# Issuing three groups of DRAM writes from GpSimd instead of SyncE in a two-layer trunk kernel

## Chip, cores and metric

The kernel runs on 1 core of one Trainium2 chip. The time is that of one execution on the device in microseconds (us). Five engines take part: TensorE (PE, with its weight loads shown as PEld), VectorE (DVE), ScalarE (ACT), GpSimd (POOL) and SyncE (SP), which here does nothing but issue DMAs.

## The reference

One layer of a streaming-encoder trunk, batch 1, 512 tokens, width 2048, hidden width 8192, all in float32. What matters here is the second half:

```
x = layer_norm(ALPHA * x + g1 * mix, ln1_g, ln1_b)      # mix: three parallel head groups
h = x * (1.0 + sc2) + sh2
ff = square(relu(h @ w_ff1)) @ w_ff2                    # 2048 -> 8192 -> 2048
x = layer_norm(ALPHA * x + g2 * ff, ln2_g, ln2_b)
```

## The kernel before

Each float32 matmul is made of three matmuls on split operands: a value is written once rounded (`wh`, by ACT) and once as the rest (`wl`, by DVE, which reads `wh`), and PE adds up wh·xh, wl·xh and wh·xl. The helper `split` does both; `act` (L57), `tt` (L60), `stt` (L63) and `load` (L127) record nearly all instructions of their engines, so one line of the profile stands for many places.

**Order.** The program doesn't write out the order of the engines' queues. A planner places the instructions of each engine before the run, by priorities (`prio`, the table `PRIO`) and by its own costs, and puts in the waits. On the chip each queue then runs strictly in that order: an instruction that waits holds up everything behind it on its engine. SP's queue holds all loads and nearly all writes; POOL's holds four `memset` (L220) and the 24 accumulating DMAs of L1365.

**First layer norm** (L993 to L1012, 870 to 960 us). Four token tiles are normalised, transposed and modulated. The modulated tile goes to `hx_d`, the normalised residual `r1[:, t]` (1 MB a tile) to `xn_d`; `base` reads `xn_d` again much later, in the second layer.

**First MLP layer** (`ff1_unit`, 960 to 1616 us). 16 blocks of 512 hidden columns. The first is done plainly, the other 15 by Strassen's scheme: seven products a block (`strassen`), each of two halves `c`, and each half of 24 matmuls on one `wh`/`wl` pair (three buffers each). A block's weights come in four loads of 1 MB into `raw`, which has four buffers: a buffer is free for the next block when the last `wl` that reads it is made. Before the products that need sums of weights, `form` makes them on DVE into `st`.

The products' results are made into four quarters `ev` (relu, square). `quarter_done` and `sums_done` put seven tiles a block into the list `waiting`, and `spread` takes one of them after each product: `put` splits it into an `hc` tile (two buffers; ACT writes the upper half, DVE the lower) and writes it, 512 KB, to `hc_d`. There are 14 such blocks. The quarters of the last two blocks are written as they are to `h_d` (256 KB, eight writes).

**Second MLP layer** (`ff2_unit` and after, from 1605 us) loads `hc_d` into `hin` (L1327), and `wff2` into `raw`; `base` loads `xn_d` into `y` (L1298). Its POOL DMAs (L1365) add a tile onto `ffa`.

The lines that the change touches:

```
nc.sync.dma_start(xn_d[t], r1[:, t])                                        # L1012
nc.sync.dma_start(hc_d[e, ORDER.index(name), :, c], w.bitcast(F32))         # L1063, in put
nc.sync.dma_start(h_d[b - 2 * NS][:, 2 * i:2 * i + 2, ...], quad2(o))       # L1081, in quarter_done
```

Of the kernel before, what the change touches and what calls it, by code (L numbers as in the profile page):

```python
# [10 lines left out]
F32 = mybir.dt.float32  # L11
# [40 lines left out]
def trunk_kernel(ctx, tc, A, out):  # L52
    nc = tc.nc
    V, S, G, T = nc.vector, nc.scalar, nc.gpsimd, nc.tensor

    def act(o, i, f=AF.Copy, **kw):
        S.activation(o, i, f, **kw)  # L57
# [7 lines left out]
    def ts(o, a, s1, s2, op0, op1=None):  # L65
        if op1 is None:
            V.tensor_scalar(o, a, s1, None, op0=op0)
        else:
            V.tensor_scalar(o, a, s1, s2, op0=op0, op1=op1)
# [11 lines left out]
    def prio(name):  # L81
        if name not in PRIO:
            name += str(stage_no[0])
        return tc.high_priority(offset=PRIO[name])

    def bank(n="mm"):
        if "two" in pools:
            return two_banks()[:, 0]
        return pools[n].tile([128, 512], F32, name=n)
# [30 lines left out]
    def split(h, l, src):  # L120
        act(h, src)
        tt(l, src, h.bitcast(F32), OP.subtract)
# [302 lines left out]
    with prio("index"):  # L425
# [23 lines left out]
        for t in range(3):  # L449
# [10 lines left out]
            for hf in range(2):  # L460
                ps = bank("sa")
                for j in range(4):
                    o = (4 * hf + j) * 128
# [465 lines left out]
    r1 = R.tile([128, NT, D], F32, name="r1")  # L929
# [13 lines left out]
    for nb in range(4):  # L943
# [17 lines left out]
        for t in range(NT):  # L961
          with prio("wo"):
            o = r1[:, t, nb * 512:(nb + 1) * 512]
# [11 lines left out]
    def ln_scalars(t):  # L975
        V.bn_aggr(out=mv[:, t, 0:2], in_=stats[:, t].rearrange("p a b -> p (a b)"))
        act(mv[:, t, 2:3], mv[:, t, 1:2], AF.Sqrt, bias=eps[:, 1:2])
        V.reciprocal(mv[:, t, 2:3], mv[:, t, 2:3])
        stt(mv[:, t, 3:4], mv[:, t, 0:1], -1.0, mv[:, t, 2:3], OP.mult, OP.mult)
# [3 lines left out]
    xn_d = dram.tile([NT, 128, D], F32, name="xn_d")  # L983

    NE, NS = 8, 7
    hc_d = dram.tile([NS, 7, 128, 2, 2, 2, 256], F32, name="hc_d")
    h_d = dram.tile([16 - 2 * NS, 128, 4, SEQ], F32, name="h_d")
# [4 lines left out]
    with prio("ln1"):  # L992
        for t in range(NT):  # L993
            ln_scalars(t)
            act(r1[:, t], r1[:, t], AF.Identity, scale=mv[:, t, 2:3], bias=mv[:, t, 3:4])
            tk = slice(t * 128, (t + 1) * 128)
            for kq in range(4):
                ps = bank(("sa", "sb")[kq % 2])
                for j in range(4):
                    k = 4 * kq + j  # L1000
                    T.transpose(ps[:, j * 128:(j + 1) * 128], r1[:, t, k * 128:(k + 1) * 128], ident)
                hf = WO.tile([128, 4, 128], F32, name="hf2", bufs=3)
                for j in range(4):
                    k = 4 * kq + j
                    o = ps[:, j * 128:(j + 1) * 128]
                    if j % 2 == 0:
                        act(hf[:, j], o, AF.Identity, scale=mod2[:, 0, k:k + 1], bias=mod2[:, 1, k:k + 1])
                    else:
                        ts(hf[:, j], o, mod2[:, 0, k:k + 1], mod2[:, 1, k:k + 1], OP.mult, OP.add)
                split(acts[:, 4 * kq:4 * kq + 4, 0, tk], acts[:, 4 * kq:4 * kq + 4, 1, tk], hf)  # L1010
                nc.sync.dma_start(hx_d[:, 4 * kq:4 * kq + 4, tk], hf)
            nc.sync.dma_start(xn_d[t], r1[:, t])  # L1012
    wo.close()
    adap.close()
    res.close()
# [39 lines left out]
    ORDER = ("b11", "b21", "n2", "t3", "n1", "t4", "b22")  # L1055

    def put(b, name, o):

        e, c = divmod(b, 2)
        w = ST.tile([128, 2, 2, 256], F32R, name="hc", bufs=2)  # L1060
        with prio("hc"):
            split(w[:, 0], w[:, 1], quad2(o))
            nc.sync.dma_start(hc_d[e, ORDER.index(name), :, c], w.bitcast(F32))  # L1063

    waiting = []

# [5 lines left out]
    def quad2(o):  # L1072
        return o.rearrange("p (m n) -> p m n", m=2)

    def quarter_done(b, i, j, o):
        if b < 2 * NS:
            if (i, j) != (0, 1):
                waiting.append(lambda: put(b, f"b{i + 1}{j + 1}", o))
        else:
            with prio("ff1"):  # L1080
                nc.sync.dma_start(h_d[b - 2 * NS][:, 2 * i:2 * i + 2, 256 * j:256 * j + 256], quad2(o))  # L1081

    def sums_done(b, o):

        if b >= 2 * NS:
            return
        b11, b22, b21, b12 = o

        def sub(dst, x, y, neg=False):
            with prio("hc"):  # L1090
                if neg:
                    stt(dst, x, -1.0, y, OP.mult, OP.subtract)
                else:
                    tt(dst, x, y, OP.subtract)

        def piece(name, *args):
            sub(*args)
            put(b, name, args[0])

        for args in (("n1", b11, b11, b12), ("t3", b12, b22, b12), ("n2", b22, b11, b22, True),  # L1100
                     ("t4", b21, b22, b21, True)):
            waiting.append(lambda args=args: piece(*args))

    o4 = []
    for i, j in QUARTERS:
        r = ev_tile()
        with prio("ff1"):
            for m in range(2):
                act(r[:, 256 * m:256 * m + 256], banks[2 * i + m][:, 256 * j:256 * j + 256], AF.Relu)
            act(r, r, AF.Square)  # L1110
        quarter_done(0, i, j, r)
        o4.append(r)
# [95 lines left out]
    def ff1_unit(b):  # L1208
# [22 lines left out]
        def done(i, j, o, ps, neg=False):  # L1231

            with prio("ff1"):
                if o is None:
                    o = ev_tile()
                    act(o, ps, AF.Relu)
                else:
                    tt(o, ps, o, OP.add)
                    act(o, o, AF.Relu, scale=-1.0 if neg else 1.0)
                act(o, o, AF.Square)  # L1240
            part[i, j] = o
            quarter_done(b, i, j, o)
# [220 lines left out]
    e = NE - 1  # L1463
# [13 lines left out]
    for t in range(NT):  # L1477
# [7 lines left out]
        for q in range(4):  # L1485
            cs_ = slice(512 * q, 512 * q + 512)
            o = ffa[:, t, cs_]
# [94 lines left out]
```

## Time and profile before

| what | value |
|---|---|
| median of 3 runs | 2275.1 us (2272.95 to 2275.82) |
| the profiled execution | 2272.37 us, of which its span 2270.6 us |
| PE busy | 2158.4 us, 95% of the span |
| DVE busy | 1876.2 us, 83% |
| ACT busy | 1098.1 us, 48% |
| POOL busy | 44.6 us, 2% |
| mean granted TensorE clock | 0.989 of full speed |
| SP's queue | 471.04 MB, 56.9% of the 16 DMA engines' time |
| POOL's queue | 12.58 MB, 3.3% |

The span runs from the first to the last instruction; the profiled execution has 1.8 us around it. An engine's queue that is blocked can be seen as a wait of the instruction at its head; a DMA has a time of issue and, where the trace has it, a time from issue to landing.

### The profile page before, as it was taken

The page shows a single profiled execution, that of the slowest core. Times are in us where ns is not written, and L with a number is a line of the kernel's source. Part 1 is how long each engine was busy: PE and PEld are TensorE (multiplying, and loading weights), DVE is VectorE, ACT ScalarE, POOL GpSimd, SP SyncE. Part 2 cuts the span into 40 slices and gives each one's busy share as a digit, 9 for nine tenths or more (in the row PEclk, how much of TensorE's full clock was granted, in tenths as well). Part 3 has the DMA queues.
Part 4 walks back from the last instruction along what each step waited for, and adds up shares of the span by engine and source line. Part 5 has one row for each costly group of instructions (what it writes and reads, how often), then busy time and mean ns, then how long its engine had stood idle before and what let it go on. Part 6 is the DMA issues. An engine that isn't in the chain of part 4 may idle for free.

```text
span 2270.6 us, 30604 instructions
## 1 busy us (share of the span) xinstructions
PE 2158.4 (95%) x11947; PEld 1845.2 (81%) x11947; DVE 1876.2 (83%) x2520; ACT 1098.1 (48%) x1572; POOL 44.6 (2%) x55
## 2 busy tenths in 40 slices
PE   6999999988889999999999999999999999999997
PEld 4778887866666787899899999999888887878886
DVE  7896899998776876788778778777699988998788
ACT  3332444448766223666555555555444443444432
POOL 0000000000000000000000000000000000000000
PEclk9999999999999999999999999999999999999999
DMA  8877563254234676735544554554788988796562
GB/s 318 315 295 288 174 228 117 95 202 151 82 107 135 239 288 254 252 135 207 202 178 177 194 185 168 204 186 142 295 307 259 342 276 275 243 333 234 149 239 86
DMA packets 129625, 485.58 MB, mean 214 GB/s; under 512 B 15556, under 2 KB 38468, under 8 KB 88264
## 3 DMA queue, kind: packets, MB, share of 16 engines
q1 hardware_dynamic: 122952, 471.04, 56.9%
q0 software_dynamic: 6528, 12.58, 3.3%
q8 instruction: 94, 1.54, 0.3%
q14 instruction: 51, 0.42, 0.1%
HBM read 392.35 MB, written 78.64 MB: 207 GB/s over the span
## 4 chain that ended last, share of the span: by engine, by line
PE 41%; DVE 34%; DMA 15%; ACT 5%; issue 4%; DVEq 0%; SPq 0%; ACTq 0%
DMA raw<-in_wff_dram 11%; DVE wl L60 11%; DVE st L60 4%; PE two L1348 4%; PE mm L197 4%; PE two L1349 4%; PE mm L198 4%; PE two L1347 4%; PE mm L196 4%; PE mm L210 3%; PE mm L208 3%; PE mm L209 3%; DVE ffa L60 2%; DVE raw L60 2%; DVE adaz L63 2%
## 5 line engine op out<-in xcount | busy, mean ns | idle before, releaser
L57 ACT ACTIVATE wh<-raw 128x1024 fp32r<-128x1024 f32 x332 | 349.2, 1057 | 408.8 <-PE two L1349 146.3
L60 DVE TENSOR_TENSOR wl<-raw,wh 128x1024 fp32r<-128x1024 f32 x332 | 402.4, 1218 | 59.8 <-ACT wh L57 59.3
L1348 PE MATMUL two<-wl,hin 128*128 128x512 f32 x784 | 309.2, 394 | 5.4 <-DVE wl L60 5.2
L1347 PE MATMUL two<-wh,hin 128*128 128x512 f32 x784 | 307.4, 392 | 3.8 <-ACT wh L57 2.1
L1349 PE MATMUL two<-wh,hin 128*128 128x512 f32 x784 | 306.8, 391 | 0.0
L203 PE MATMUL mm<-acts,wl 128*128 128x256 f32 x720 | 208.6, 290 | 23.8 <-DVE wl L60 23.8
L196 PE MATMUL mm<-acts,wh 128*128 128x512 f32 (+1 forms) x568 | 221.6, 394 | 7.2 <-ACT ve L57 3.8
L197 PE MATMUL mm<-acts,wl 128*128 128x512 f32 (+1 forms) x568 | 223.3, 393 | 1.1 <-DVE wl L60 0.9
L198 PE MATMUL mm<-acts,wh 128*128 128x512 f32 (+1 forms) x568 | 221.2, 390 | 0.0
L63 DVE SCALAR_TENSOR_TENSOR adaz<-raw,cols,adaz 128x1024 f32<-128x1024 f32 (+2 forms) x180 | 198.1, 1111 | 11.7 <-DMA raw<-in_adaR_dram 8.8
L202 PE MATMUL mm<-acts,wh 128*128 128x256 f32 x720 | 204.9, 285 | 1.7 <-ACT ev L57 1.7
L204 PE MATMUL mm<-acts,wh 128*128 128x256 f32 x720 | 204.8, 284 | 0.0
L203 PE MATMUL mm<-tx,wl 128*128 128x256 f32 x720 | 203.9, 283 | 0.0
L204 PE MATMUL mm<-tx,wh 128*128 128x256 f32 x720 | 203.2, 282 | 0.0
L202 PE MATMUL mm<-tx,wh 128*128 128x256 f32 x720 | 202.0, 281 | 0.0
L1348 PEld LDWEIGHTS two<-wl,hin 128*128 128x128 f32 x784 | 147.9, 189 | 45.6 <-DVE wl L60 14.5
L1347 PEld LDWEIGHTS two<-wh,hin 128*128 128x128 f32 x784 | 147.9, 189 | 36.1 <-ACT wh L57 3.0
L209 PE MATMUL mm<-wl,acts 128*128 128x512 f32 x448 | 175.0, 391 | 1.2 <-DVE wl L60 1.0
L210 PE MATMUL mm<-wh,acts 128*128 128x512 f32 x448 | 174.9, 391 | 0.0
L208 PE MATMUL mm<-wh,acts 128*128 128x512 f32 x448 | 174.1, 392 | 0.3 <-DVE z_t L60 0.2
L1349 PEld LDWEIGHTS two<-wh,hin 128*128 128x128 f32 x784 | 148.0, 189 | 30.2
L203 PEld LDWEIGHTS mm<-acts,wl 128*128 128x128 f32 x720 | 139.2, 193 | 30.9 <-DVE wl L60 30.7
(316 smaller groups left out, 4534.9 us busy)
## 6 DMA issues: line engine op xcount, KB each, us to landing
raw<-in_wff_dram SPq DMA_DIRECT2D x128, 1024.0 KB, 6.7
hc_d<-hc SPq DMA_DIRECT2D x98, 512.0 KB, 4.2
hin<-hc_d SPq DMA_DIRECT2D x49, 1024.0 KB, 9.0
raw<-in_adaR_dram SPq DMA_DIRECT2D x48, 1024.0 KB, 5.1
raw<-in_adaS_dram SPq DMA_DIRECT2D x32, 1024.0 KB, 9.4
raw<-in_wo_dram SPq DMA_DIRECT2D x16, 1024.0 KB, 7.0
araw<-in_adaR_dram SPq DMA_DIRECT2D x16, 1024.0 KB, 6.3
raw<-in_wconv_dram SPq DMA_DIRECT2D x12, 1024.0 KB, 5.1
```

What stands on the lines that cost most here:

```text
L57: S.activation(o, i, f, **kw)
L60: V.tensor_tensor(o, a, b, op=op)
L63: V.scalar_tensor_tensor(o, a, s, b, op0=op0, op1=op1)
L196: T.matmul(ps, wh, xh, start=start, stop=False)
L197: T.matmul(ps, wl, xh, start=False, stop=False)
L198: T.matmul(ps, wh, xl, start=False, stop=stop)
L202: T.matmul(ps, wh, xh, start=start, stop=False, skip_group_check=True)
L203: T.matmul(ps, wl, xh, start=False, stop=False, skip_group_check=True)
L204: T.matmul(ps, wh, xl, start=False, stop=stop, skip_group_check=True)
L1347: T.matmul(ps[:, t], xh, h[:, k], start=first, stop=False, skip_group_check=True)
L1348: T.matmul(ps[:, t], xh, l[:, k], start=False, stop=False, skip_group_check=True)
L1349: T.matmul(ps[:, t], xl, h[:, k], start=False, stop=last, skip_group_check=True)
```

## The change

The instructions that issue three groups of writes move from SP's queue to POOL's: the four of `xn_d`, the 98 of `hc_d` and the eight of `h_d`. Sources, targets, sizes and buffers stay. `G` is `nc.gpsimd`. A DMA that POOL issues goes through another DMA queue (software_dynamic in the profile) than one that SP issues (hardware_dynamic).

```
                 split(acts[:, 4 * kq:4 * kq + 4, 0, tk], acts[:, 4 * kq:4 * kq + 4, 1, tk], hf)
                 nc.sync.dma_start(hx_d[:, 4 * kq:4 * kq + 4, tk], hf)
-            nc.sync.dma_start(xn_d[t], r1[:, t])
+            G.dma_start(xn_d[t], r1[:, t])
...
             split(w[:, 0], w[:, 1], quad2(o))
-            nc.sync.dma_start(hc_d[e, ORDER.index(name), :, c], w.bitcast(F32))
+            G.dma_start(hc_d[e, ORDER.index(name), :, c], w.bitcast(F32))
...
             with prio("ff1"):
-                nc.sync.dma_start(h_d[b - 2 * NS][:, 2 * i:2 * i + 2, 256 * j:256 * j + 256], quad2(o))
+                G.dma_start(h_d[b - 2 * NS][:, 2 * i:2 * i + 2, 256 * j:256 * j + 256], quad2(o))
```

## Rows read from the trace of the kernel before

**Rows 1.** The page, busy us, share of the span, instructions:
```profile
PE 2158.4 (95%) x11947; PEld 1845.2 (81%) x11947; DVE 1876.2 (83%) x2520; ACT 1098.1 (48%) x1572; POOL 44.6 (2%) x55
```

**Rows 2.** Waits of PE, 990 to 1616 us: total, times, longest:
```profile
PE mm L203 <- DVE wl L60: 23.8, 34, 3.4
```

**Rows 3.** Waits of SP's queue, same stretch and columns:
```profile
SPq L1063 <- DVE hc L60: 312.3, 68, 13.2
SPq L127 <- DVE wl L60: 219.0, 58, 11.3
```

**Rows 4.** Timeline of SP, 1228 to 1266 us: start, length, what:
```profile
1247.25 2.67 SPq L127 DMA_DIRECT2D raw<-in_wff_dram  x2
1249.97 0.93 SPq L1063 DMA_DIRECT2D hc_d<-hc  x2
1260.80 1.47 SPq L127 DMA_DIRECT2D raw<-in_wff_dram  x2
1265.25 0.33 SPq L1063 DMA_DIRECT2D hc_d<-hc  x1
```

**Rows 5.** Timeline of DVE, same stretch; in brackets the idle before:
```profile
1246.01 1.22 DVE L60 TENSOR_TENSOR wl<-raw,wh 128x1024 fp32r<-128x1024 f32 x1
...
1247.75 0.68 DVE L60 TENSOR_TENSOR hc<-ev,hc 128x512 fp32r<-128x512 f32 x1
...
1249.85 0.69 DVE L60 TENSOR_TENSOR hc<-ev,hc 128x512 fp32r<-128x512 f32 x1 [0.29 <-ACT hc L57]
...
1257.15 1.23 DVE L60 TENSOR_TENSOR st<-raw 128x1024 f32<-128x1024 f32 x1 [3.68 <-DMA raw<-in_wff_dram]
...
1259.55 2.35 DVE L60 TENSOR_TENSOR wl<-raw,wh 128x1024 fp32r<-128x1024 f32 x2
```

**Rows 6.** The chain that ended last, 1242 to 1276 us: start, length, what:
```profile
1249.59 7.48 DMA raw<-in_wff_dram
...
1261.93 9.08 DMA raw<-in_wff_dram
```

**Rows 7.** Timeline of PE, 1259 to 1262 us:
```profile
1260.82 0.39 PE L203 MATMUL mm<-acts,wl 128*128 128x256 f32 x1 [1.39 <-DVE wl L60]
```

**Rows 8.** DMA issues: count, KB each, median us from issue to landing:
```profile
hc_d<-hc SPq DMA_DIRECT2D x98, 512.0 KB, 4.2
...
xn_d<-r SPq DMA_DIRECT2D x4, 1024.0 KB, 3.9
...
h_d<-ev SPq DMA_DIRECT2D x8, 256.0 KB, 3.8
```

**Rows 9.** Line 1365 (POOL's DMAs): ns min/median/max, and landing:
```profile
L1365 POOL DMA_DIRECT2D ffa<-c x24: 1200/1200/1329, 1706.0 to 2142.7; - x24
...
DMA to landing us min/median/max: 5.3/6.6/14.7
```

**Rows 10.** Windows: us, busy by engine, clock, DMA share, GB/s:
```profile
2136.83:2138.33 1.50, 1.50 (x8) 1.23 (x8) 0.82 (x1) 0.75 (x2) 1.20 (x1) 1.00 0.00 0
```

**Rows 11.** Line 1365, the one DMA issued at 1988.8 us, loads about it:
```profile
DMA to landing us min/median/max: 13.6/13.6/13.6
```

**Rows 12.** Timeline of ACT, 1228 to 1266 us:
```profile
1241.91 0.63 ACT L57 ACTIVATE hc<-ev 128x512 fp32r<-128x512 f32 x1 [1.45 <-DMA hc_d<-hc]
1243.20 0.63 ACT L57 ACTIVATE hc<-ev 128x512 fp32r<-128x512 f32 x1 [0.66 <-DMA hc_d<-hc]
1243.74 1.04 ACT L57 ACTIVATE wh<-raw 128x1024 fp32r<-128x1024 f32 x1
```

**Rows 13.** Windows, columns as in rows 10:
```profile
1132.00:1137.00 5.00, 4.58 (x21) 4.58 (x22) 3.92 (x5) 1.89 (x3) 0.00 (x0) 0.50 0.73 246
```

**Rows 14.** Timeline of SP, 1600 to 1640 us:
```profile
1616.07 0.39 SPq L1081 DMA_DIRECT2D h_d<-ev  x1
1616.50 0.96 SPq L1298 DMA_DIRECT2D y<-xn_d  x2
```

**Rows 15.** Timeline of POOL, 1600 to 1720 us:
```profile
1613.86 0.95 POOL L220 MEMSET adaz<- 128x1024 f32 x1 [778.40 <-PE mm L204]
```

## The prediction

> **What bounds the kernel now.** I read the page first, then the waits stage by stage, then the timelines of one block of the first MLP layer side by side. PE is busy for 95% of the span [rows 1]. In the first MLP layer, 626 us long, its main wait is 23.8 us in 34 pieces, all for DVE's `wl` [rows 2]. So at most about 1% of the kernel can be won there; there is no such bound on what can be lost.
>
> SP is where the change acts, and its waits look like an invitation: its queue stood 312.3 us behind writes of `hc_d` that waited for DVE's half of the tile [rows 3]. Whether that cost anything depends on what stood behind those writes. The second row answers: the weight loads, once at the head of the queue, waited another 219.0 us for DVE's `wl`, 58 times [rows 3], and the 15 blocks have 60 loads. Nearly every load is held by its own buffer, which is free when the last `wl` that reads it is made. The write ahead of it had gone by then.
>
> One block shows the loop. DVE makes a `wl` from 1246.01 us, 1.22 us long, and SP issues the first load of a pair at 1247.25, as that ends; the second load waits for the next `wl` and goes at 1249.59 [rows 4 to 6]. It lands 7.48 us later, and DVE, idle for 3.68 us, starts `st` at 1257.15. Two `wl` stand behind it in DVE's order and begin at 1259.55; PE starts on the first at 1260.82, after 1.39 us of idling [rows 5 to 7]. The second pair goes at 1260.80, with the same pattern, and its last load takes 9.08 us [rows 4, 6]. The loads' landings lie on the path; their issue, as far as SP's order goes, does not.
>
> **What is removed.** 110 issues leave SP: 98 of `hc_d`, four of `xn_d`, eight of `h_d` [rows 8]. No load becomes free sooner, because `raw` still has four buffers and the same `wl` frees them. Two writes gain something: one `hc` tile is ready at 1247.75 + 0.68 = 1248.43 but is issued at 1249.97, behind a load that waits [rows 4, 5]. It gains 1.5 us that nobody needs, since that buffer is next written in the following pair's stretch. The gain is taken as 0; were a load held by a write in some block, it would be worth that write's wait for that one load.
>
> **What is added on POOL.** Its DMA instructions take 1200 ns, median and minimum alike, under a busy DVE [rows 9]. 98 of them in some 560 us are 118 us of work for an engine that idles 778.40 us there [rows 15]: no cost in itself. What could cost is the latency to landing, since ACT may not refill an `hc` buffer before its write has landed. On SP a lone write lands in about 2.6 us: ACT is let go by one at 1241.91 and by the next at 1243.20 [rows 12]. Those 1.29 us apart, for two writes issued close together, I take as the time that 512 KB need on the DMA engines. For POOL the nearest row is an accumulating DMA of the same size: 5.3 us at best [rows 9], which reads its target too. In the first 1.5 us after such an issue the DMA engines moved nothing [rows 10]. With 1.5 us before the first byte, 1.3 us of data and some 0.5 us to land I estimate 3.3 us, about 0.8 us more than on SP; bounds 2.6 and 5.3 us. What would be late is ACT's `wh` at 1243.74, ready at 1244.78; the `wl` that reads it starts at 1246.01 because DVE is busy until then [rows 5, 12]. That leaves 1.2 us of cover, so 0.8 us cost nothing. At 5.3 us the cover is gone: late by 2.7 us, less 1.2, 1.5 us a block, 21 us over 14 blocks.
>
> A page's rule would add something else here. The Trainium skill (SBUF — State Buffer, section "SBUF: two separate sides") has it that a DMA issued by GpSimd starves for descriptors while DVE runs an instruction in its two-port mode. By that rule such a DMA would be slow in its issue; the trace speaks against it for this DVE work, with 1200 ns at the median and 1329 ns at most [rows 9], and the sum stays.
>
> **What is moved to another queue.** This is the term I cost. On SP the two writes that follow the first pair of loads stand behind both loads in the same queue. From POOL they come through a queue of their own, while the loads are in flight. The first would be issued at 1248.43 and bring bytes about 1.5 us later, at 1250; the second is ready at 1249.85 + 0.69 = 1250.54, with bytes from 1252 [rows 5, 10]. The pair's last load lands at 1257.07, so 5 us of it are still to come. If the writes wait behind the loads as now, the cost is 0. If they all go ahead of the loads' last bytes, it is 2 × 1.3 = 2.6 us. The trace of the second layer shows the sharing: a POOL DMA among loads took 13.6 us in place of 5.3 [rows 9, 11], so loads already queued mostly go first. I am nearer the lower end and take a quarter, 0.65 us. The write after the second pair is ready 3.3 us after that pair's second load was issued (1265.25 against 1261.93) [rows 4, 6] and comes 1.5 us later still; bounds 0 and 1.3, taken 0. There are 14 blocks of seven writes, so 13 first pairs have two writes behind them: 13 × 0.65 = 8.5 us. It goes to PE in full, because PE already waits at that point [rows 7].
>
> The Trainium skill (DMA: Bandwidth & Descriptors, "Issuing engines are not separate DMA queues") states that DMAs of all issuing engines run on the same 16 DMA engines and interleave, and that issuing from several saves only issue time. That rule speaks against a gain from the move. The 13.6 us agree with it.
>
> **The rest.** `xn_d`: four writes of 1 MB that nobody reads until 1616 us [rows 8, 14]; 0. `h_d`: the last write stands just ahead of the `y` loads at 1616.50 [rows 14], so these could go up to 0.4 us sooner. But POOL's `memset`, now at 1613.86 [rows 15], may come to stand behind that write, and then end 1616.07 + 1.2 + 0.95 = 1618.2, against 1614.81 before, holding up SP's queue behind it for up to 3 us. Bounds −0.4 and +3, once; taken 0.
>
> **Sum.** 8.5 us on the profiled execution's 2272.4 gives 2280.9. The median of the runs lies 2.7 us higher than that execution, so the forecast is 2275.1 + 8.5, about 2283 us. What a measurement of this kernel can tell from no change is about 0.2%, 4.6 us.
>
> **Rivals.** *Nothing happens* (0.27): the writes' packets queue up behind loads that are already there, as most of the 13.6 us suggest. Time 2275 us. Against it: one write arrives just as the second load is issued.
>
> *The planner turns the order* (0.21, faster). It places by its own costs, and SP's queue is lighter by 110 instructions. PE waits because two `wl`, whose `wh` are there, stand behind a `st` that waits for a load [rows 5, 7]. It decides as soon as one `wl` stands ahead of that `st`. Half of the 23.8 us [rows 2] is 12 us: 2263 us. For it: nothing in the data forbids that order. Against: the same priorities and the same buffers as before.
>
> *The `hc` ring* (0.10, slower): landing 5.3 us, 21 us and the 8.5: 2305 us. For it: that row is the only one there is. Against: those DMAs read their target.
>
> *The clock* (0.04, slower): PE's longest wait of 3.4 us [rows 2] is followed by 5 us at a granted clock of 0.50, that is 1.2 GHz [rows 13], which cost 2.5 us; the other waits left the clock up. It decides if the load term is at its upper end: 1.39 + 2.6 = 4.0 us of idling at each pair. 13 × (2.6 + 2.5) = 66 us: 2341 us.
>
> **Chances.** The forecast has 0.38. Its own range, from 0.2 to 1.3 us a pair, is 2278 to 2292 us, so a little of it is within 0.2%. Faster 0.22, same 0.30, slower 0.48. The range 2263 to 2305 us reaches to the planner's case below and the ring's above, and leaves out the clock's and the far halves of those two.
>
> **What the profile would show.** Right: loads that wait for `wl` as long as before or longer, the second load of the first pair landing 0.5 to 1 us later, DVE's wait ahead of `st` and PE's ahead of `wl` longer by that, POOL at 1.2 us an issue, and `hc` waits of ACT longer without `wl` being late. Wrong: loads issued earlier against their `wl`; a landing from POOL of 5 us with `wl` late behind ACT; PE's wait at `wl` gone with another order on DVE; or a gain outside the first MLP layer.

## The result and the profile after

The changed kernel takes 2293.39 us (median of 6 runs, 2286.28 to 2302.54); the kernel before took 2272.85 us (6 runs, 2269.45 to 2275.82) beside it. The ratio is 1.0097, with a 95% interval of 1.0074 to 1.0120: about 22 us slower. The profiled execution took 2294.82 us, with a span of 2293.1 us. Below, a ratio's part above 1 is turned into microseconds with 2272 us.

The page's busy row, which answers to [rows 1]:

```profile
PE 2170.1 (95%) x11947; PEld 1861.1 (81%) x11947; DVE 1876.5 (82%) x2520; ACT 1100.0 (48%) x1572; POOL 104.5 (5%) x165
```
The same number of matmuls keeps PE busy 11.7 us longer. Where that happened is seen in windows over the first MLP layer, from its first matmul to its last, in the kernel before and in the changed one (columns as in [rows 10]):

```profile
971.60:1614.00 642.40, 617.01 (x5040) 609.35 (x5040) 508.20 (x531) 367.15 (x480) 0.14 (x1) 0.99 0.52 185
```
```profile
980.40:1640.40 660.00, 624.96 (x5040) 619.89 (x5040) 509.95 (x532) 368.97 (x480) 57.27 (x106) 0.97 0.49 180
```

The layer is 17.6 us longer. PE idles 660.00 - 624.96 = 35.0 us in it, against 25.4 before, so 9.6 us are waiting. The other 8.0 us are the same 5040 matmuls at a lower mean clock, 0.97 in place of 0.99. The layer starts 8.8 us later and what follows it is 3.9 us shorter; the runs below separate those parts better than two profiled executions do.

The first two Strassen blocks of the kernel before, then those of the changed kernel and the twelve blocks behind them:

```profile
971.60:1055.00 83.40, 81.23 (x671) 80.74 (x672) 70.05 (x74) 48.45 (x66) 0.00 (x0) 1.00 0.53 183
```
```profile
980.40:1076.20 95.80, 86.88 (x671) 85.87 (x672) 76.70 (x82) 52.20 (x73) 8.50 (x16) 0.93 0.48 176
1076.20:1599.70 523.50, 497.53 (x4035) 493.67 (x4034) 408.09 (x429) 295.40 (x381) 45.42 (x85) 0.98 0.49 180
```

In these two executions the first two blocks are 12.4 us longer and the twelve behind them 6.3 us (they took 517.2 us before; that line stands below, beside `form_pool`). Of the 8.0 us of slower matmuls, 5.7 us lie in the first two.

PE's waits in the layer, 960 to 1645 us (answers to [rows 2]). Those for `wl` are fewer and longer, and those for ACT's `ev` and `wh` have grown, from 1.7 us in all before:

```profile
PE mm L203 <- DVE wl L60: 27.1, 19, 3.9
PE mm L202 <- ACT ev L57: 5.8, 2, 4.7
PE mm L202 <- ACT wh L57: 2.9, 2, 2.6
```

SP's queue, 990 to 1616 us (answers to [rows 3]): the write that stood in front is gone, and the waiting has gone over to the loads, which still wait for `wl`.

```profile
SPq L127 <- DVE wl L60: 616.7, 57, 32.3
```

One block in the middle. SP's timeline has loads only ([rows 4]):

```profile
1263.29 16.20 SPq L127 DMA_DIRECT2D raw<-in_wff_dram  x4
```

POOL's timeline; the writes at 1264.99 and 1266.88 are those that follow the first pair of loads:

```profile
1264.99 0.53 POOL L1063 DMA_DIRECT2D hc_d<-hc  x1 [3.17 <-ACT ev L57]
1266.88 0.53 POOL L1063 DMA_DIRECT2D hc_d<-hc  x1 [1.36 <-DVE hc L60]
```

The chain, for the pair's second load ([rows 6]), then DVE ([rows 5]) and PE ([rows 7]):

```profile
1265.63 8.63 DMA raw<-in_wff_dram
```
```profile
1262.04 1.22 DVE L60 TENSOR_TENSOR wl<-raw,wh 128x1024 fp32r<-128x1024 f32 x1
...
1274.38 1.23 DVE L60 TENSOR_TENSOR st<-raw 128x1024 f32<-128x1024 f32 x1 [4.88 <-DMA raw<-in_wff_dram]
...
1276.79 2.35 DVE L60 TENSOR_TENSOR wl<-raw,wh 128x1024 fp32r<-128x1024 f32 x2
```
```profile
1278.06 0.39 PE L203 MATMUL mm<-acts,wl 128*128 128x256 f32 x1 [2.25 <-DVE wl L60]
```

The steps are those of before, and the waits are longer. The first load goes at 1263.29, as the `wl` of 1262.04 ends. The second takes 8.63 us in place of 7.48, DVE waits 4.88 us ahead of `st` in place of 3.68, and PE 2.25 us ahead of `wl` in place of 1.39. From the first load's issue to `st` it is 1274.38 - 1263.29 = 11.1 us. Worked out in the same way, the median of the fourth to the fourteenth Strassen block is 9.4 us before and 11.1 us after for the first pair, and 9.5 and 8.8 us for the second.

The clock. Three more of PE's waits after the change, and the granted clock in windows behind that of 1278.06 and these three:

```profile
1323.54 0.38 PE L203 MATMUL mm<-acts,wl 128*128 128x256 f32 x1 [3.93 <-DVE wl L60]
...
1410.15 0.58 PE L203 MATMUL mm<-acts,wl 128*128 128x256 f32 x1 [2.65 <-DVE wl L60]
...
1586.81 0.38 PE L203 MATMUL mm<-acts,wl 128*128 128x256 f32 x1 [1.75 <-DVE wl L60]
```
```profile
1278.00:1281.40 3.40, 3.34 (x28) 3.34 (x29) 2.87 (x4) 1.56 (x3) 0.00 (x0) 1.00 0.67 219
1325.00:1328.00 3.00, 3.00 (x16) 3.00 (x16) 2.05 (x3) 1.95 (x4) 0.00 (x0) 0.50 0.89 363
1410.20:1413.30 3.10, 3.10 (x14) 3.10 (x15) 2.77 (x3) 1.37 (x3) 0.00 (x0) 0.50 0.67 209
1587.60:1590.60 3.00, 3.00 (x16) 3.00 (x15) 2.02 (x3) 1.26 (x2) 0.49 (x1) 0.50 0.90 330
```

After waits of 3.93, 2.65 and 1.75 us PE ran at 0.50, that is 1.2 GHz; after the one of 2.25 us it kept 2.4 GHz. The length of the one wait just before doesn't tell which it will be.

### The profile page after: what moved, and what is told of

Its sections match the earlier page's. It is cut to its first block, busy times and chain, and to the rows that moved or that the text cites. A ratio compares the mean times of both kernels' runs of the same rounds, so it can differ in the third digit from the quotient of the medians.

```text
span 2293.1 us, 30633 instructions
## 1 busy us (share of the span) xinstructions
PE 2170.1 (95%) x11947; PEld 1861.1 (81%) x11947; DVE 1876.5 (82%) x2520; ACT 1100.0 (48%) x1572; POOL 104.5 (5%) x165
## 4 chain that ended last, share of the span: by engine, by line
PE 49%; DVE 22%; DMA 14%; issue 9%; ACT 5%; POOL 0%; SPq 0%; DVEq 0%; ACTq 0%; POOLq 0%
DMA raw<-in_wff_dram 8%; DVE wl L60 7%; PE two L1348 5%; PE two L1349 4%; PE two L1347 4%; PE mm L197 4%; PE mm L210 4%; PE mm L198 4%; PE mm L209 4%; PE mm L208 4%; PE mm L196 4%; DMA hc_d<-hc 2%; DVE st L60 2%; DVE ffa L60 2%; DVE adaz L63 2%
## 5 line engine op out<-in xcount | busy, mean ns | idle before, releaser
L196 PE MATMUL mm<-acts,wh 128*128 128x512 f32 (+1 forms) x568 | 224.1, 398 | 10.5 <-ACT ve L57 3.8
L198 PE MATMUL mm<-acts,wh 128*128 128x512 f32 (+1 forms) x568 | 224.1, 396 | 0.0
L202 PE MATMUL mm<-acts,wh 128*128 128x256 f32 x720 | 209.3, 291 | 5.8 <-ACT ev L57 5.8
L204 PE MATMUL mm<-acts,wh 128*128 128x256 f32 x720 | 209.0, 290 | 0.0
```

The costliest lines, as they stand in the source:

```text
L196: T.matmul(ps, wh, xh, start=start, stop=False)
L198: T.matmul(ps, wh, xl, start=False, stop=stop)
L202: T.matmul(ps, wh, xh, start=start, stop=False, skip_group_check=True)
L204: T.matmul(ps, wh, xl, start=False, stop=stop, skip_group_check=True)
```

## Experiments

All were run in five rounds beside the kernel before. Each edit is shown against that kernel, unless another is named.

### Which group of writes

```
hc_only       L1063:  G.dma_start(hc_d[...], ...)          # xn_d and h_d stay on SP
xn_h_only     L1012, L1081 on G                            # hc_d stays on SP
first2_pool   L1063:  (G if b < 2 else nc.sync).dma_start(hc_d[...], ...)
first2_sp     the changed kernel, with L1063:  (nc.sync if b < 2 else G).dma_start(...)
```

`hc_only`:

> Only the 98 writes of hc_d move to POOL; xn_d and h_d stay on SP. ACT's and DVE's order differs from that of the kernel before only in the first blocks of the first MLP layer. If the loss lies in the hc_d writes (loads of the first pair of each block landing 1.5 to 2 us later, and the hc ring in the first two dense blocks), this keeps most of it: +14 to +20 us against the kernel before, blocks 3 to 14 at 43.5 to 44.5 us each. If the loss is in the residual writes and the first layer norm, whose start lay 7 us later in the changed kernel's profile, this is within 5 us of the kernel before.

2286.32 us; ratio 1.0074, 1.0059 to 1.0089.

`xn_h_only`:

> Only the four xn_d and eight h_d writes move to POOL; all hc_d writes stay on SP. If the loss lies in the hc_d writes: within 5 us of the kernel before, blocks at 42.5 to 43 us, the first pair of loads at 9.1 us from the first issue to the last landing. If the layer norm's part or the planner's new order costs, 6 to 9 us slower, and the transposes start 5 us or more later than at 902.5 us.

2274.09 us; ratio 1.0023, 1.0009 to 1.0036.

`first2_pool`:

> hc_d writes of the first two blocks from POOL, those of the other twelve from SP; xn_d and h_d on SP. PE, ACT and DVE have the same order as in hc_only, so the two differ by the queue of the later writes alone. If loads and writes share the DMA engines from two queues at the cost of the loads: the first pair of loads is back at 9.1 us in the later blocks and the kernel is 12 to 18 us faster than hc_only; it is then 0 to 12 us slower than the kernel before by the first two blocks. If the planner's order is what costs, it equals hc_only.

2274.89 us; ratio 1.0027, 1.0012 to 1.0041.

`first2_sp`:

> The mirror image: xn_d and h_d on POOL, hc_d of the first two blocks on SP, of the other twelve on POOL. The order on PE, ACT and DVE is nearly that of xn_h_only. If the sharing costs 1.5 us a block: 12 to 18 us slower than xn_h_only, first pairs at 10.5 to 11 us. If only the dense first two blocks cost (two hc buffers, writes landing 6 to 9 us after issue): equal to xn_h_only, and 10 us or more faster than the changed kernel.

2285.73 us; ratio 1.0076, 1.0057 to 1.0094.

The planner makes new orders when an issue moves, so only kernels with the same order are compared closely. `hc_only` and `first2_pool` have the same order on PE, ACT and DVE; they differ by the writes of the 12 later blocks: 0.47%, 10.7 us. `first2_sp` and `xn_h_only` have nearly the same order and differ by the same writes: 0.53%, 12.0 us. So these writes cost about 11 us, 0.9 us a block, in either setting. The first two blocks add 0.27% (6 us), `xn_d` and `h_d` 0.23% (5 us). The three parts make 0.97 to 1.03%, against the 0.97% of the whole change.

The 6 us of the first two blocks are what is left over. In the profiled execution of `first2_pool` they take 93.6 us in place of 83.4, but the twelve blocks behind them, whose writes go from SP as before, are 7.9 us shorter than the 517.2 us of the kernel before:

```profile
1070.60:1579.90 509.30, 491.46 (x4035) 485.34 (x4034) 407.88 (x430) 292.87 (x381) 0.00 (x0) 1.00 0.51 185
```

So blocks behind a delay can win part of it back. Why was not tried.

### Which writes in the later blocks

```
two_pool    L1063:  (G if b >= 2 and name in ("t4", "b11") else nc.sync).dma_start(...)
five_pool   ... b >= 2 and name not in ("t4", "b11") ...
t4_pool     ... b >= 2 and name == "t4" ...
b11_pool    ... b >= 2 and name == "b11" ...
```

`t4` and `b11` are the two writes that follow the first pair of loads.

> From block 2 of hidden columns on, only the two hc_d writes a block that become ready while the first pair of loads is in flight (t4, and b11 of the next block) go through POOL; all other writes stay on SP. PE, ACT and DVE keep the order of the kernel before but for some rows of the first blocks. If it is these two writes, sharing the DMA engines with the loads, that cost: the first pair takes 10.5 to 11.3 us instead of 9.3, and nearly the whole loss of the twelve later blocks is here, +9 to +13 us against the kernel before. If the cost is POOL's longer way to a landing (the hc ring), which the other five writes feel, it is 0 to +3 us.

2284.63 us; ratio 1.0069, 1.0047 to 1.0092. From first issue to `st` the first pair takes 10.6 us (median as above), in `hc_only` 11.1.

> The complement: from block 2 on, the other five hc_d writes a block go through POOL, t4 and b11 stay on SP behind the loads. Same order on PE, within a few rows on ACT and DVE. If sharing with the first pair of loads is the cost: first pair at 9.1 to 9.5 us, 0 to +2 us against the kernel before. If the ring is the cost: ACT's hc waits for hc_d longer by 0.8 us each and +9 us or more.

2273.32 us; ratio 1.0017, 1.0002 to 1.0033. Two writes carry the loss; the other five cost at most a third of a per cent, and the first pair is nearly as before (9.65 us against 9.4). By its median `two_pool` loses more than was expected and more than the seven writes together (0.69% against 0.47 to 0.53%), though its interval reaches down to 0.47%. The second pair takes 8.7 us in `five_pool` and 9.3 in `two_pool`, so its gain in the changed kernel goes with the other five writes.

> Half the dose: only t4, the first of the two writes, goes through POOL, with the same order on PE, ACT and DVE as in two_pool. If the loss is in proportion to the bytes that overtake the loads: first pair about 10.1 us and half of the loss of two_pool, +5 us. If the granted clock makes the larger part of it (PE waits of about 2 us and more are followed by 3.4 us and more at half clock), the waits stay below that and the loss is under a third, +1 to +3 us, with no more stretches at half clock in the first MLP layer than before.

2280.28 us; ratio 1.0045, 1.0028 to 1.0062. That is about two thirds of the loss of `two_pool`, more than either side expected, and the first pair takes 10.5 us. The clock is not needed for it: in the profiled execution the 5040 matmuls of the layer take 616.29 us, against 617.01 before. Nor do waits of about 2 us and more always bring half the clock, as the expectation has it: in the changed kernel one of 2.25 us didn't and one of 1.75 us did.

```profile
977.32:1625.00 647.68, 616.29 (x5040) 609.41 (x5040) 508.42 (x531) 367.71 (x480) 6.73 (x13) 0.99 0.50 184
```

> Only the second of the two writes that follow the first pair of loads (b11) goes from POOL, in the 12 later blocks; the engines' orders are those of the run with both writes and of the run with t4 alone. If the two costs add up, this one is the rest: 14.6 - 10.3, about +4 us against the kernel before (about 2277). The second write is issued some 2 us later, so less of the loads is left to be held up. The rival: each write alone already costs most of it, because what counts is that a second queue is served at all beside the loads: about +10 us (2283). First pair, first issue to DVE's st: about 10.0 us by the first, 10.5 or more by the rival.

2277.48 us; ratio 1.0028, 1.0013 to 1.0042. The orders of `two_pool`, `t4_pool` and `b11_pool` are the same. By their ratios `t4` costs 0.69 - 0.28 = 0.41% (9 us), and `b11` 0.69 - 0.45 = 0.24% (5 us); 0.04% is left over. Within the intervals, which are some 0.2% to either side, they add up, and the rival's 2283 us is outside that of `b11_pool`. By the medians the first write, issued just ahead of the second load, costs nearly twice the second. The profiled execution of `b11_pool` shows little of its part: from first issue to `st` the pair takes 9.4 us, as before and not the 10.0 expected, and its span of 2270.2 us is the shortest of its twelve.

What happens to such a write is seen in one block of each kernel. Before, SP issues the first load at 1247.25, the second at 1249.59, and `t4` at 1249.97; it lands 8.4 us later (line 1063 in a window about that issue), at 1258.4. The second load has landed at 1257.07 [rows 6]:

```profile
L1063 SPq DMA_DIRECT2D hc_d<-hc x1: 424/424/424, 1250.0 to 1250.0; - x1
...
DMA to landing us min/median/max: 8.4/8.4/8.4
```

In `t4_pool` POOL issues the same write at 1252.88, and it takes 8.8 us (the same view), to 1261.7; the second load is on the chain:

```profile
DMA to landing us min/median/max: 8.8/8.8/8.8
```
```profile
1253.51 8.70 DMA raw<-in_wff_dram
```

It lands at 1262.21, after the write. The two have changed places. Among loads the write takes 8.4 us from SP and 8.8 from POOL. But seen from the second load, POOL issues it a us sooner, and the two queues move their bytes side by side. From 1257 to 1260 us, first SP's queue and then POOL's (packets, MB, share of the DMA engines' time):

```profile
q1 hardware_dynamic: 113, 0.82, 77.4%
q0 software_dynamic: 68, 0.26, 21.3%
```

The load's delay of 8.70 - 7.48 = 1.2 us is about the 1.29 us that the prediction read as the time of 512 KB. Over the later blocks, where the trace has the landing, the second load takes 6.75 us at the median before, 7.2 in `b11_pool`, 8.1 in `t4_pool` and 8.5 in the changed kernel. Whether POOL matters here, or any second queue would do the same, was not tried: no run issued these writes from an engine other than SP and POOL.

### The first two blocks

```
(G if b == 1 else nc.sync).dma_start(hc_d[e, ORDER.index(name), :, c], w.bitcast(F32))   # L1063
```

> The hc writes of the second block alone go from POOL. If POOL's later landing is what makes the first two blocks 6 us longer (ACT's waits for the hc ring 5.8 us each in place of 2.6), this block has its part of it: about +3 us against the kernel before (2275), with waits of ACT for the ring of 4 to 6 us in this block and 2 to 3 us in the first one. The rival: it is the other order that the planner makes of these blocks; then the ring's waits don't follow the queue, and are long or short in both blocks alike, wherever the writes are issued.

2277.30 us; ratio 1.0025, 1.0008 to 1.0042: some 6 us where 3 were expected, as much as `first2_pool` with both blocks. ACT's waits for the `hc` ring (the two `hc` buffers in turn) in the first Strassen block (979 to 1021 us, writes on SP) and in the second (1021 to 1072 us, writes on POOL):

```profile
ACT hc L57 <- DMA hc_d<-hc: 4.2, 3, 1.9
```
```profile
ACT hc L57 <- DMA hc_d<-hc: 16.1, 6, 7.1
```

The waits follow the queue. The first block takes 41.8 us and the second 51.0; before they took 42.1 and 41.4. The chain through the second, 1036 to 1072 us, has two writes as its longest pieces:

```profile
1039.12 9.51 DMA hc_d<-hc
1048.72 0.63 ACT hc L57
1049.35 0.96 ACT wh L57
...
1056.46 8.25 DMA hc_d<-hc
...
1065.33 1.05 ACT wh L57
```

SP issued four loads from 1037.66 us on. The write of 1039.12 came among them and took 9.51 us; ACT stood at the next `hc`, and the `wh` behind it in ACT's queue was late for PE, which waited 4.9 us for `wh` in this block. In the changed kernel the chain through the first two blocks, 980 to 1077 us, has the same pieces:

```profile
1000.80 6.71 DMA hc_d<-hc
...
1015.23 7.50 DMA hc_d<-hc
...
1047.72 8.65 DMA hc_d<-hc
1056.46 0.63 ACT hc L57
1057.09 0.96 ACT wh L57
```

The kernel before has a write of 8.66 us on its chain there too, but its ring waits come to 10.6 us in eight pieces, against 23.4 us in seven. POOL's way to a landing is not the longer one here. Line 1063 in the first two blocks, before and after, where the trace has the landing:

```profile
DMA to landing us min/median/max: 2.6/7.5/9.7
```
```profile
DMA to landing us min/median/max: 2.9/3.9/9.2
```

What has grown is ACT's waiting for the late ones. The order of these blocks also changed with the queue, so how much of the 6 us is the ring alone stays open.

### `xn_d` alone

```
-            nc.sync.dma_start(xn_d[t], r1[:, t])
+            G.dma_start(xn_d[t], r1[:, t])
```

> Only the four residual writes xn_d move to POOL. Nobody waits for them, but the planner turns the order of the layer norm stage. If that order costs the 5 us seen when xn_d and h_d moved together: +4 to +6 us, with a longer PE wait at the transposes and the first block at 46 us instead of 42. If the 5 us lie with h_d at the end of the layer: 0 to +1 us.

2276.10 us; ratio 1.0030, 1.0014 to 1.0046. These four writes alone cost what they cost with `h_d`, so `h_d` costs nothing that can be measured. They land nearly as fast from POOL as from SP (line 1012 in this kernel; before, 3.9 us at the median [rows 8]), the last of them over 40 us before the first MLP layer's first matmul:

```profile
L1012 POOL DMA_DIRECT2D xn_d<-r x4: 532/547/715, 904.9 to 927.6; - x4
...
DMA to landing us min/median/max: 4.3/4.3/5.2
```

What differs is the order that the planner made of ACT's and DVE's work around them. The first Strassen block takes 45.8 us in place of 42.1, and PE's longest wait in it has grown (before, 971.6 to 1013.7 us; `xn_only`, 976 to 1022 us):

```profile
PE mm L202 <- ACT ev L57: 1.7, 2, 1.3
```
```profile
PE mm L202 <- ACT ev L57: 3.8, 2, 2.4
```

That the order is the cause is argued from this, not tried: no run had the old order with `xn_d` on POOL, so a delay of the transfers beside these writes isn't excluded.

### The sums of weights on POOL

`st` stands in DVE's queue ahead of two `wl`. Made on POOL, it can't hold them up.

```
             with prio("w_split"):
-                tt(new_s(c, "s1"), w4[c]["a21"], w4[c]["a22"], OP.add)
-                tt(new_s(c, "s2"), w4[c]["s1"], w4[c]["a11"], OP.add)
+                add = G.tensor_tensor if late else tt
+                add(new_s(c, "s1"), w4[c]["a21"], w4[c]["a22"], OP.add)
+                add(new_s(c, "s2"), w4[c]["s1"], w4[c]["a11"], OP.add)
```

`late` is true in the first MLP layer alone. `form_pool` does this to the kernel before, `after_form_pool` to the changed one.

> The kernel before, with the sums of weights (form, the st tiles of the first MLP layer that read raw) made on POOL instead of DVE, so that no st that waits for a load stands ahead of a wl on DVE. By the theory that the loads' landing reaches PE through that st, PE's wait at wl falls from 23.8 us to less than half, and the time to about 2263 us. The rival: PE's wait doesn't hang on that st but on the loads themselves or on ACT's wh, or POOL's additions slow DVE down: no change, or slower by up to 20 us (2272 to 2295).

2269.68 us; ratio 0.9991, 0.9976 to 1.0005: no difference that can be measured. But it is made of two that can be seen. In the third to the fourteenth Strassen block, first the kernel before and then `form_pool` (windows, columns as above):

```profile
1055.10:1572.30 517.20, 494.73 (x4035) 488.17 (x4033) 411.62 (x435) 296.19 (x386) 0.00 (x0) 0.99 0.51 186
```
```profile
1072.10:1573.60 501.50, 488.12 (x4035) 484.97 (x4034) 443.65 (x384) 298.02 (x384) 140.79 (x49) 1.00 0.53 190
```

These blocks are 15.7 us shorter: 9.1 us less idling of PE, and 6.6 us less for the same 4035 matmuls. But PE's wait for `wl` falls there from 23.0 to 13.2 us, not to less than half, and about half of the 15.7 us may have another cause: in `first2_pool` the same blocks are 7.9 us shorter with nothing changed in them. So the theory that the landing reaches PE through that `st` is supported in part. The first two blocks take 94.9 us in place of 83.5, in another order, and take back most of the gain; the expected 2263 us was missed for that. The additions themselves are slow on POOL, 2.6 to 3.2 us against 1.23 us on DVE.

> The changed kernel, with form on POOL as well. POOL's queue then holds the writes behind additions that wait for the loads, so most writes stand behind the loads again, as they did on SP. By the theory that the loss is the writes' bytes among the first pair's loads, the loss of 20 us falls by half or more against the kernel with form on POOL alone (within 10 us of it). The rival: the loss comes from POOL's latency through the hc ring, and writes that wait behind additions make it worse: 20 us or more above the kernel with form on POOL alone.

2283.02 us; ratio 1.0053, 1.0030 to 1.0076. Against `form_pool` the writes on POOL cost 0.62%, 14 us, in place of 22. That is a third less by the medians, where half or more was expected, and the mechanism was wrong. The writes were not held back behind the loads: from first issue to last landing, where the trace has it, the first pair takes 11.5 us here and 9.1 in `form_pool`. They lengthen the loads at least as much as in the changed kernel. Over the layer of the profiled executions PE idles 9.3 us more than in `form_pool`, much like the 9.6 us without `form` on POOL, but the same matmuls take 2.2 us longer and not 8.0. What is less is mostly the part of the clock.

## Why the prediction was right, and where its sum was off

The forecast was 2283 us; the time is 2293.4, inside the range, and the kernel is slower by more than 0.2%. The main mechanism is shown: with the two writes that follow the first pair left on SP, and the other five on POOL, most of the loss in the later blocks is gone. That the time fell inside the range is in part luck: the loss is about 22 us where 8.5 were forecast, and about half of it comes from places that the sum put at nothing. The range had the room for the `hc` ring's case. Four terms were mis-sized.

**The loads' term: 8.5 us, measured about 11.** The quarter of 2.6 us was too low. The first pair takes 1.7 us longer, two thirds of the upper bound. The second pair gives 0.7 us back, with the other five writes on POOL; why was not tried. That leaves about 1 us a block, which agrees with the 0.9 us of the runs. The prediction's bounds for one write were 0 and 1.3 us; by the second load's time to landing the first write comes out near 1.3, the second near a third of that. Not all of it reached PE, as the sum had it: in the block shown DVE waits 1.20 us longer and PE 0.86. The 13.6 us of [rows 11] had been taken as loads that go first; but a write that lands late is no sign that the loads beside it don't.

**The clock: chance 0.04, and it carries part of the loss.** It was thought to decide from 4.0 us of idling at each pair. Waits of 1.75 to 3.93 us were followed by 1.2 GHz, in some blocks and not in others, and 8.0 us of the layer's 17.6 are matmuls at the lower clock, most of them in the first two blocks. So it isn't a case beside the others but comes on top of the waits of any of them. The load term stands without it as well: `t4_pool` loses some 10 us with matmuls no longer than before.

**The `hc` ring: 0 us, measured up to 6 in two blocks.** In the later blocks the step holds. A lone write from POOL lands in 2.92 us:

```profile
1299.63 2.92 DMA hc_d<-hc
```

The estimate was 3.3, and ACT's two waits for the ring grow from 1.45 and 0.66 us [rows 12] to

```profile
1258.56 0.63 ACT L57 ACTIVATE hc<-ev 128x512 fp32r<-128x512 f32 x1 [1.93 <-DMA hc_d<-hc]
1259.95 0.63 ACT L57 ACTIVATE hc<-ev 128x512 fp32r<-128x512 f32 x1 [0.76 <-DMA hc_d<-hc]
```

with no wait of PE's behind them in that block. But the prediction read one block and counted 14 like it. In the first two the writes stand closer together and meet the loads; those on the chains land after 6.7 to 9.5 us, beyond the 5.3 us that was taken as the upper bound, and the 1.2 us of cover are gone. From SP such a landing took up to 9.7 us too, so what was missed is the meeting with the loads and not a slower way from POOL. That the ring is all of it isn't shown, since the order changed as well.

**`xn_d`: 0 us, measured 5 to 7 us.** That nobody reads it until 1616 us holds. What was left out is that moving an issue makes the planner place the neighbours anew; that this is what costs is argued, not tried. The rival "the planner turns the order" had this step, but as a gain in the later blocks; the order there is the same from about the fourth block on, and it turned in the first ones.

**Right as put:** no load became free sooner (SP waits for `wl` 616.7 us); no run shows a cost of POOL's issue, or one of `h_d`; the gain at the end of the write's wait on SP was 0. POOL's issue was mis-sized without effect: 533 ns at the mean, not 1200.

```profile
L1063 POOL DMA_DIRECT2D hc_d<-hc x98 | 52.2, 533 | 590.5 <-DVE hc L60 352.4 <-ACT ev L57 155.6 <-ACT wh L57 79.3
```

The Trainium skill (SBUF — State Buffer, "SBUF: two separate sides") has GpSimd's descriptors starve while DVE runs an instruction in its two-port mode; 98 issues at 533 ns, with DVE busy for 82% of the span, show nothing of it. No run here shows whether any of that work is in this mode, so they neither bear out the rule nor speak against it, and the prediction's reading of [rows 9] as evidence against it went too far. The Trainium skill's rule that DMAs of all issuing engines interleave on the same engines (DMA: Bandwidth & Descriptors, "Issuing engines are not separate DMA queues") agrees with `t4_pool`, where both queues moved bytes side by side and the write and the load behind it changed places.

## What to carry to other kernels

A queue that is blocked for 312 us may cost nothing: ask what stands behind its head, and what that would wait for next. A shared queue also gives an order, here loads ahead of writes, and splitting it lets the write take the DMA engines at just the moment when a load is on the path. Read the densest block of a loop as well as a typical one, and where a planner places the work, count on a moved issue turning the order around it.

A version that may beat both kernels was not run: the sums of weights on POOL for the later blocks only, with all writes on SP. If the first two blocks then keep their 83.5 us, up to 15.7 us could be won in the later blocks, or about half of that if the rest came from the delay ahead of them.

## What the runs showed of the hardware

- A plain DMA of 512 KB issued by POOL costs it 533 ns at the mean, less than half of the 1200 ns of the accumulating ones [rows 9], and its lone landing of 2.92 us is only some 0.3 us later than the 2.6 us read from SP.
- A write of 512 KB issued from POOL 0.6 us ahead of a load of 1 MB, with another such load under way, lands 0.5 us before it, and the load takes 1.2 us longer to land than with the write behind it on SP. The write's own latency is about the same from both queues: 8.8 and 8.4 us. In 3 us in which both had bytes to move, SP's queue moved 0.82 MB and POOL's 0.26 MB (`t4_pool`).
- PE waits of 3.93, 2.65 and 1.75 us were followed by windows of some 3 us at 1.2 GHz; one of 2.25 us was not.
- An addition of two 128x1024 tiles in float32 takes 2.6 to 3.2 us on POOL (`form_pool`), against 1.23 us on DVE:

```profile
L1161 POOL TENSOR_TENSOR st<-st,raw 128x1024 f32<-128x1024 f32 x30 | 94.6, 3152 | 4.6 <-DVE acts L60 2.4
L1160 POOL TENSOR_TENSOR st<-raw 128x1024 f32<-128x1024 f32 x30 | 78.0, 2599 | 557.2 <-DMA raw<-in_wff_dram 393.1 <-DVE st L63 137.5 <-DVE wl L60 26.6
```
